# Where six modulation vectors of a two-layer trunk are made: one moves from attention into the channel mixer

## The chip, the cores and the metric

The kernel runs as one program on one core of a Trainium2 chip. The core has five instruction queues. TensorE (PE; its weight loads are listed apart as PEld) multiplies matrices and transposes. VectorE (DVE), ScalarE (ACT) and GpSimd (POOL) work element by element. SyncE (SP) issues nearly all transfers between the core and device memory. Each queue runs its instructions in the order in which they were put there, and an instruction that waits holds up everything behind it on its queue. The metric is the device time of one execution, in microseconds (us).

## What is computed

The reference is a trunk of two layers on a sequence of 1024 tokens and 1024 features. Each layer has a token mixer (layer 0: attention with a forget gate, 16 heads; layer 1: gated linear attention) and a channel mixer (SwiGLU with 2816 hidden features). Every part is normalised and then shifted, scaled and gated by six vectors, which come from one conditioning vector `c` and one matrix per layer:

```
c_act = silu(c)
for i in range(2):
    mod = c_act @ ada_w[i] + ada_b[i]            # 1024 x 6144 matrix, 24 MB per layer
    sh1, sc1, g1, sh2, sc2, g2 = split(mod, 6)   # six vectors of 1024
    h = rms_norm(x, norm1_g[i]) * (1 + sc1) + sh1
    y = attention(h) if i == 0 else gated_linear_attention(h)
    x = x + g1 * y
    h = rms_norm(x, norm2_g[i]) * (1 + sc2) + sh2
    gate, up = split(h @ ffn_w_in[i], 2)
    x = x + g2 * ((silu(gate) * up) @ ffn_w_out[i])
out = rms_norm(x, final_g)
```

This document numbers the vectors of a layer 0 to 5, as the code does (`j`): 0 and 1 are the first norm's shift and scale, 2 is the token mixer's gate, 3 and 4 are the second norm's shift and scale, 5 is the channel mixer's gate. "The sixth" is j = 5. The vectors depend on nothing but `c`, so they can be made at any time before their use.

## The kernel before

**Precision and tiling.** Every large product is made of three matmuls on float32r halves: a value is split in a high part (a ScalarE copy) and a low part (a VectorE or GpSimd subtraction), and `mm3` (lines 316 to 318) multiplies high by high, high by low and low by high. Activations lie with features on the 128 partitions and tokens along the free axis, in halves of 512 tokens. The two channel mixers use one level of Strassen's scheme (seven products instead of eight); a product there (`prod`) is twelve matmuls of 128x512.

**Attention of layer 0.** Eight pairs of heads, `p` = 0 to 7. While the scores, softmax and outputs of pair `p` run (`attention(p)`), the projections of pair `p+1` run between them: queries and keys (`qk_proj`, on TensorE `qk_b`) and, up to p = 5, values (`v_half`, `vps_b`). A generator pair is interleaved by given weights (`weave`), and a scheduler then puts the instructions on each engine's queue by its own estimate of times. In the softmax of one block of 128 queries, VectorE adds the gate sums and takes the minimum (line 1298), ScalarE exponentiates and sums (1302), VectorE takes the reciprocal of the sum (1303), GpSimd multiplies (1304), TensorE transposes (1324), ScalarE and VectorE split the transposed block (174, 175, `pt_s`), and TensorE multiplies it with the values (1338). VectorE also evacuates queries (869, 871) and keys (883, 884: `KLA`, `KLB`) and splits a quarter of the weights (246).

**How a modulation vector is made beside this work.** There are three makers, each a generator that is advanced a little at a time by a pacing counter (`Pace`):

- `ada_steps` with four tiles a step (attention): one step loads 512 KB of the matrix by four transfers of 128 KB (line 453) into a buffer of the ring `wr`, which the weights use too (three buffers), and VectorE multiplies and adds it to a sum in four instructions of 128x256 (line 516; the first of a vector is line 514). Eight steps make a vector. `ada0(t)` advances it by `t` steps after each of the projections `qk_proj` from p = 2 on.
- `ada_steps` with two tiles a step (channel mixers and the second token mixer): 256 KB by four transfers of 64 KB, two VectorE instructions of 128x256, sixteen steps a vector. A step costs `ADA_A + ADA_B` units of the counter, and each `prod` gives it 2.56. Buffers are its own: three of 256 KB in the channel mixers, with loads two steps ahead.
- `ada_pool` (attention): GpSimd makes one vector with a multiplication (477) and an addition (479) for each tile, from one buffer of its own.

At the end of a vector `ada_end` sums its parts by four small matmuls (459) on TensorE and adds the bias on VectorE (462). For j = 1 and 4, `make_a` then combines it with the norm's weight (444).

**Where the twelve vectors are made.** Layer 0: j = 0 and 1 at the start, j = 2, 3 and 4 by VectorE in attention, j = 5 by GpSimd in attention. Layer 1: j = 0 and 1 in the channel mixer of layer 0 (`mid(0, 1)`), j = 2, 3 and 4 in the gated linear attention, j = 5 in its own channel mixer. Layer 0's j = 2 is first used when attention's output is added to the stream (1442), j = 3 and 4 at the norm of the channel mixer, and j = 5 at the end of the channel mixer (1901 and 1928).

**The channel mixer's flow.** `mid()` is called once the two halves of the normalised input have been formed. Then twenty groups of seven products follow, each adding to running sums by VectorE (1670); five PSUM buffers take the products in turn, and the weights of up to five products ahead are split by ScalarE (174) and VectorE (175). Hidden values are split again (1548, 1549) and written out (1601) to be read back as tiles for the second matrix (1785). Before the last two groups `ada1.flush()` runs whatever is left of the vectors.

Of the kernel before, what the change touches and what calls it, by code (L numbers as in the profile page):

```python
# [53 lines left out]
def trunk(ctx, tc, x, c, ada_w, ada_b, norm1_g, norm2_g, ffn_w_in, ffn_w_out,  # L54
# [412 lines left out]
    def ada_pool(l, j, acc, raw):  # L467

        raw = raw.rearrange("p (t c) -> p t c", t=2)
        ada_load(raw, l, j, 0, 2)  # L470
        yield 1.0
        for n in range(16):
            for t in range(2):
                o = 32 + t * 16 + n
                y = raw[:, t] if n or t else acc
                with tc.issue_after(last_of("G")):
                    nc.gpsimd.tensor_scalar(y, raw[:, t], c42[:, o:o + 1], 1.0, op0=ALU.mult, op1=ALU.mult)
                    if n or t:
                        nc.gpsimd.tensor_add(acc, acc, y)
                if t and n < 15:  # L480
                    ada_load(raw, l, j, n + 1, 2)
                yield 1.0
        ada_end(l, j, acc)
        yield 1.0
# [61 lines left out]
    def ada1_queue(js, acc, raws_):  # L546
        r = Cycle(raws_)
        for j in js:
            ada1.q.append(ada_steps(1, j, acc, r, 2, len(raws_) - 1))

    mk = mrows[2]
    nc.vector.memset(mk, 0.0)
# [704 lines left out]
    def qk_proj(p, i):  # L1257

        if i == 0:
            qkt[p] = qk_tiles(p)  # L1260
        wt = feed.next()
        feed.depth = 3
        for hf in range(2):
            ps = pj([P, HALF], F32, f"qk{i}{p}{hf}")
            yield from proj(ps, wt, hT, hf)
            (k_evac if i else q_evac)(ps, qkt[p], hf)
        if p > 1:
            ada0(2.4)

    oTs = {}  # L1270

# [110 lines left out]
            yield from g  # L1382

    acc0 = acc_r([P, 2, HALF], F32, "acc0")
    ada0p.q.append(ada_pool(0, 5, acc0[:, 0, 256:512], acc0[:, 1]))
    acc0 = acc0[:, 0, 0:256]
    for j in (2, 3, 4):
        ada0.q.append(ada_steps(0, j, acc0, wr, 4, 0))
    run(v_half(0, 0, gates_end))
    q_evac(accs[1][1][1], qkt[0], 1)  # L1390
# [614 lines left out]
        ada1_queue(js, v[0][:, 0:256], v[1:4])  # L2005
        ada1.at -= 20.0

    ADA_A, ADA_B = 6.0, 3.0
    ffn(0, oh, xs, slots, "fo", lambda: mid(0, 1), norm_mixer)
    h1 = hs1  # L2010
    after_norm = marks.pop("G0")
    split_after.update(marks)
# [17 lines left out]
    athl = Ring(big, take(1))  # L2030
    s_slot, on_slot = take(2)
    ada_v = Views(take(2), 2, [HALF], "ad").v
    ada1_queue((2, 3, 4), ada_v[0][:, 0:256], ada_v[1:3])
    ADA_A, ADA_B = 2.6, 1.0
    nba = cst.tile([P, 4], F32, name="nba")
    nc.vector.tensor_scalar(nba, vec[:, P + 16:P + 20], -1.0, None, op0=ALU.mult)
# [494 lines left out]
        return fzs[hf]()  # L2531

    ADA_A, ADA_B = 12.0, 6.0
    ffn(1, None, xs, slots, "go", lambda: mid(5), final_norm, final_scale, (out_blocks, out_ends))
    dump("xb1", xs)

# [28 lines left out]
```

## Time and profile before

Three runs took 2346.65 us (median), 2345.26 and 2350.23. The profiled execution took 2348.03 us; its span from the first to the last instruction was 2346.3, so 1.7 us lie outside it. The granted TensorE clock was 0.995.

| Engine | busy, us | share of the span | instructions |
|---|---|---|---|
| TensorE (PE) | 2326.5 | 99% | 12168 |
| TensorE weight loads (PEld) | 1983.7 | 85% | 12168 |
| VectorE (DVE) | 1779.5 | 76% | 2947 |
| ScalarE (ACT) | 1123.0 | 48% | 2166 |
| GpSimd (POOL) | 1142.8 | 49% | 1005 |

Stages, by the instructions in the timeline: the start until about 125 us, attention of layer 0 until about 600, its channel mixer until about 1300, gated linear attention until about 1630, its channel mixer to the end.

A row of groups reads: line, engine, operation, tile written `<-` tiles read, shapes, count | busy time, mean ns of one | idle time of the engine just before them and what ended it. A row of waits reads: engine, line `<-` what it waited for: total us, how often, longest. A row of the timeline reads: start, duration, engine, line, operation, tiles, shapes, count, and in brackets the engine's idle time before it with what ended it. `SPq` is a transfer's issue. A row of stretches gives, for each engine, the busy time in that stretch and its instructions, then the granted clock, the DMA engines' busy share and GB/s.

### The profile page before, as it was taken

Reading aid. Unit: us, or ns where it says so; the run is one execution under the profiler, and the core shown is the slowest. Engines: PE = TensorE matmul, PEld = TensorE weight load, DVE = VectorE, ACT = ScalarE, POOL = GpSimd, SP = SyncE. Lnnn points to the kernel's source line nnn. Section 1 sums busy time; section 2 is a strip of 40 time slices with the busy share of each in tenths; the row PEclk is TensorE's granted clock in tenths of the full one; section 3 lists DMA queues with packets and bytes.
Section 4 is the critical chain, followed back from the end, with each engine's and each line's share of the span. In section 5 each row is a group of like instructions: output and inputs, shape, how many; then the busy total and the mean of one; then the engine's idle time right before and its main releaser. Section 6 shows DMA issues by size and latency. Waiting matters only on the chain.

```text
span 2346.3 us, 35561 instructions
## 1 busy us (share of the span) xinstructions
PE 2326.5 (99%) x12168; PEld 1983.7 (85%) x12168; DVE 1779.5 (76%) x2947; ACT 1123.0 (48%) x2166; POOL 1142.8 (49%) x1005
## 2 busy tenths in 40 slices
PE   8999999999999999999999999999999999999999
PEld 7988888888888888888888899898888888888888
DVE  6577787877687888887788666568787777876787
ACT  6565665665544333345325654345444333345236
POOL 1334455533345656665563522335456666664651
PEclk8999999999999999999999999999999999999999
DMA  8423333432325545448774443554435544458774
GB/s 262 146 79 116 108 113 94 128 127 103 117 95 188 184 162 167 161 172 314 253 272 155 134 129 100 148 174 167 150 106 160 177 150 156 140 189 299 238 267 137
DMA packets 349615, 383.38 MB, mean 163 GB/s; under 512 B 25373, under 2 KB 286649, under 8 KB 349433
## 3 DMA queue, kind: packets, MB, share of 16 engines
q1 hardware_dynamic: 349432, 381.11, 49.3%
q8 instruction: 96, 1.57, 0.3%
q14 instruction: 87, 0.70, 0.1%
HBM read 279.76 MB, written 101.25 MB: 162 GB/s over the span
## 4 chain that ended last, share of the span: by engine, by line
PE 90%; DVE 3%; DMA 3%; issue 1%; SPq 1%; ACT 1%; POOL 1%; DVEq 0%; POOLq 0%; ACTq 0%
PE p_b L316 16%; PE p_b L318 16%; PE p_b L317 16%; PE o_b L1338 2%; PE t_b L1324 2%; PE qk_b L316 2%; PE qk_b L317 2%; PE qk_b L318 2%; PE vps_b L318 1%; PE vps_b L316 1%; PE vps_b L317 1%; PE gr_b L316 1%; PE s_b L1292 1%; PE s_b L1293 1%; PE gr_b L317 1%
## 5 line engine op out<-in xcount | busy, mean ns | idle before, releaser
L174 ACT CAST o_s<-xv_s 128x512 fp32r<-128x512 f32 (+1 forms) x392 | 236.5, 610 | 344.4 <-PE p_b L318 256.9
L175 DVE TENSOR_TENSOR o_s<-xv_s,o_s 128x512 fp32r<-128x512 f32 (+1 forms) x392 | 335.2, 860 | 42.6 <-ACT o_s L174 40.5
L318 PE MATMUL p_b<-B,o_s 128*128 128x512 f32 x608 | 236.0, 389 | 0.0
L317 PE MATMUL p_b<-B,o_s 128*128 128x512 f32 x608 | 235.9, 389 | 0.0
L316 PE MATMUL p_b<-B,o_s 128*128 128x512 f32 x608 | 235.4, 390 | 0.0
L1304 POOL TENSOR_SCALAR lp_s<-lp_s,st 128x128 f32<-128x128 f32 (+7 forms) x128 | 98.2, 771 | 246.1 <-DVE st L1303 231.2
L951 POOL TENSOR_TENSOR ex_s<-xv_s,xv_s 128x512 f32<-128x512 f32 (+1 forms) x64 | 95.6, 1494 | 238.3 <-DMA xv_s<-in_ffn_w_in_dram 118.4
L316 PE MATMUL p_b<-T,o_s 128*128 128x512 f32 x480 | 186.8, 389 | 0.0
L317 PE MATMUL p_b<-T,o_s 128*128 128x512 f32 x480 | 186.7, 389 | 0.0
L318 PE MATMUL p_b<-T,o_s 128*128 128x512 f32 x480 | 181.2, 389 | 0.0
L318 PEld LDWEIGHTS p_b<-B,o_s 128*128 128x128 f32 x608 | 114.1, 188 | 23.9
L316 PEld LDWEIGHTS p_b<-B,o_s 128*128 128x128 f32 x608 | 114.1, 188 | 23.7 <-DVE x L1670 0.2
L317 PEld LDWEIGHTS p_b<-B,o_s 128*128 128x128 f32 x608 | 114.2, 188 | 23.5
L1302 ACT ACTIVATE lp_s<-lp_s,st 128x128 f32<-128x128 f32 (+7 forms) x128 | 99.4, 777 | 57.2 <-DVE st L1298 55.8
L953 POOL TENSOR_TENSOR xv_s<-ex_s,xv_s 128x512 f32<-128x512 f32 (+1 forms) x64 | 94.5, 1477 | 58.9 <-DVE o_s L175 55.9
L1670 DVE TENSOR_TENSOR ex_s<-ex_s,p_b 128x512 f32<-128x512 f32 x140 | 94.2, 681 | 36.7 <-PE p_b L318 36.6
L174 ACT CAST pt_s<-t_b 128x512 fp32r<-128x512 f32 (+1 forms) x160 | 79.7, 547 | 73.7 <-PE t_b L1324 73.1
L963 POOL TENSOR_TENSOR xv_s<-xv_s,xv_s 128x512 f32<-128x512 f32 x48 | 65.5, 1365 | 92.7 <-issue 52.3
L246 POOL TENSOR_TENSOR w_l_s<-w__s,w_h_s 128x256 fp32r<-128x256 f32 x90 | 69.4, 800 | 84.3 <-ACT w_h_s L242 66.3
L175 DVE TENSOR_TENSOR pt_s<-t_b,pt_s 128x512 fp32r<-128x512 f32 (+1 forms) x160 | 96.3, 630 | 15.9 <-ACT pt_s L174 15.4
L318 PEld LDWEIGHTS p_b<-T,o_s 128*128 128x128 f32 x480 | 90.1, 188 | 18.7
L317 PEld LDWEIGHTS p_b<-T,o_s 128*128 128x128 f32 x480 | 90.1, 188 | 18.7
(1527 smaller groups left out, 7413.9 us busy)
## 6 DMA issues: line engine op xcount, KB each, us to landing
xv_s<-in_ffn_w_in_dram SPq DMA_DIRECT2D x176, 256.0 KB, 3.2
hid_B<-x SPq DMA_DIRECT2D x66, 512.0 KB, 2.8
ad_s<-in_ada_w_dram SPq DMA_DIRECT2D x384, 64.0 KB, 2.4
hid_T<-x SPq DMA_DIRECT2D x44, 512.0 KB, 2.9
xv_s<-in_ffn_w_out_dram SPq DMA_DIRECT2D x88, 256.0 KB, 3.8
ada_s<-in_ada_w_dram SPq DMA_DIRECT2D x96, 128.0 KB, 2.7
T2o<-hid_T SPq DMA_DIRECT2D x22, 512.0 KB, 6.6
T1o<-hid_T SPq DMA_DIRECT2D x22, 512.0 KB, 6.3
```

What stands on the lines that cost most here:

```text
L174: nc.scalar.copy(hi, src)
L175: nc.vector.tensor_sub(lo, src, hi.bitcast(F32))
L246: (nc.gpsimd if i < 3 else nc.vector).tensor_sub(lo[:, cs], rw[:, cs], hi[:, cs].bitcast(F32))
L316: nc.tensor.matmul(ps, ah, bh, start=start, stop=False, skip_group_check=chain)
L317: nc.tensor.matmul(ps, ah, bl, start=False, stop=False, skip_group_check=chain)
L318: nc.tensor.matmul(ps, al, bh, start=False, stop=stop, skip_group_check=chain)
L951: nc.gpsimd.tensor_add(s1, a21, a22)
L953: nc.gpsimd.tensor_sub(a11, s1, a11)
L963: nc.gpsimd.tensor_sub(r[A12], r[A12], r[A11])
L1302: nc.scalar.activation(lp, lp, AF.Exp, bias=mcur, scale=-1.0, accum_out=st[:, qi, 2:3])
L1304: nc.gpsimd.tensor_scalar(lp, lp, st[:, qi, 3:4], 1.0, op0=ALU.mult, op1=ALU.mult)
L1670: nc.vector.tensor_add(d, d if src is None else dest(G, src), ps)
```

## The change

Layer 0's j = 5 is no longer made in attention. GpSimd makes j = 4 there in its place, by the same instructions, and VectorE makes only j = 2 and 3, at 1.6 steps per call where it had 2.4. The channel mixer of layer 0 makes three vectors where it had made two: layer 0's j = 5 first, then layer 1's j = 0 and 1. A step's price there falls from 6 + 3 to 4 + 2 units, so that 48 steps take as many units (288) as 32 did. The argument of `mid` and `ada1_queue` now counts over both layers (5 is layer 0's j = 5; 6 and 7 are layer 1's 0 and 1), which is all that the other two places of the diff say.

```diff
@@ ada1_queue
-            ada1.q.append(ada_steps(1, j, acc, r, 2, len(raws_) - 1))
+            ada1.q.append(ada_steps(*divmod(j, 6), acc, r, 2, len(raws_) - 1))
@@ qk_proj
         if p > 1:
-            ada0(2.4)
+            ada0(1.6)
@@ before the attention
-    ada0p.q.append(ada_pool(0, 5, acc0[:, 0, 256:512], acc0[:, 1]))
+    ada0p.q.append(ada_pool(0, 4, acc0[:, 0, 256:512], acc0[:, 1]))
     acc0 = acc0[:, 0, 0:256]
-    for j in (2, 3, 4):
+    for j in (2, 3):
         ada0.q.append(ada_steps(0, j, acc0, wr, 4, 0))
@@ channel mixer of layer 0
-    ADA_A, ADA_B = 6.0, 3.0
-    ffn(0, oh, xs, slots, "fo", lambda: mid(0, 1), norm_mixer)
+    ADA_A, ADA_B = 4.0, 2.0
+    ffn(0, oh, xs, slots, "fo", lambda: mid(5, 6, 7), norm_mixer)
@@ gated linear attention
-    ada1_queue((2, 3, 4), ada_v[0][:, 0:256], ada_v[1:3])
+    ada1_queue((8, 9, 10), ada_v[0][:, 0:256], ada_v[1:3])
@@ channel mixer of layer 1
-    ffn(1, None, xs, slots, "go", lambda: mid(5), final_norm, final_scale, (out_blocks, out_ends))
+    ffn(1, None, xs, slots, "go", lambda: mid(11), final_norm, final_scale, (out_blocks, out_ends))
```

The scheduler places the rest of attention anew around the missing steps, so the order of instructions moves there on all engines. Three places follow, all on VectorE.

The first is in attention, where the queries of pair 6 are about to be evacuated (the reciprocal at its end belongs to a block of 640 keys). `ada_s` are the loaded pieces of the matrix, `acc_s` the sum, `lp_s` the scores, `st` their minimum and sum, `pt_s` the transposed block. Before:

```order
L175 TENSOR_TENSOR pt_s_94_4711<-t_b_94_4706,pt_s_94_4711 128x512
L516 SCALAR_TENSOR_TENSOR acc_s_1_749<-ada_s_45_4791,c_164,acc_s_1_749 128x256 x3
L516 SCALAR_TENSOR_TENSOR acc_s_1_749<-ada_s_47_5084,c_164,acc_s_1_749 128x256 x4
L1298 ISA lp_s_62_4758,st_4760<-s_b_117_4761,cum_s_10_4058 128x384
L1298 ISA st_4760 128x1
L175 TENSOR_TENSOR pt_s_95_4728<-t_b_95_4724,pt_s_95_4728 128x384
L1298 ISA lp_s_62_4758,st_4760<-s_b_118_4765,cum_s_10_4058,st_4760 128x256
L1298 ISA st_4760 128x1
L516 SCALAR_TENSOR_TENSOR acc_s_1_749<-ada_s_48_5093,c_164,acc_s_1_749 128x256
L175 TENSOR_TENSOR pt_s_96_4823<-t_b_96_4818,pt_s_96_4823 128x512
L516 SCALAR_TENSOR_TENSOR acc_s_1_749<-ada_s_48_5093,c_164,acc_s_1_749 128x256
L1303 RECIPROCAL st_4760<-st_4760 128x1
```

Now:

```order
L175 TENSOR_TENSOR pt_s_94_4666<-t_b_94_4661,pt_s_94_4666 128x512
L1298 ISA lp_s_62_4713,st_4715<-s_b_117_4716,cum_s_10_4013 128x384
L1298 ISA st_4715 128x1
L1298 ISA lp_s_62_4713,st_4715<-s_b_118_4720,cum_s_10_4013,st_4715 128x256
L1298 ISA st_4715 128x1
L175 TENSOR_TENSOR pt_s_95_4683<-t_b_95_4679,pt_s_95_4683 128x384
L1303 RECIPROCAL st_4715<-st_4715 128x1
```

Nine instructions of the modulation vector (three, four, one and one) have left the queue ahead of the reciprocal.

The second is one pair of heads later, where keys are evacuated (`KLA`, `KLB`) and the first weights of attention's output matrix are split (`wo_0l_s`). Before:

```order
L516 SCALAR_TENSOR_TENSOR acc_s_1_749<-ada_s_56_5927,c_164,acc_s_1_749 128x256 x2
L1303 RECIPROCAL st_5377<-st_5377 128x1
L516 SCALAR_TENSOR_TENSOR acc_s_1_749<-ada_s_56_5927,c_164,acc_s_1_749 128x256
L1298 ISA lp_s_73_5441,st_5442<-s_b_139_5443,cum_s_12_4846 128x384
L1298 ISA st_5442 128x1
L246 TENSOR_TENSOR wo_0l_s_54_5650<-wo_0_s_54_5647,wo_0h_s_53_5649 128x256
L883 TENSOR_TENSOR KLA_4859<-qk_b_42_5481,KA_4857 64x512
L884 TENSOR_TENSOR KLB_4860<-qk_b_42_5481,KB_4858 64x512
L1298 ISA lp_s_73_5441,st_5442<-s_b_140_5451,cum_s_12_4846 128x512
```

Now:

```order
L1303 RECIPROCAL st_5319<-st_5319 128x1
L1298 ISA lp_s_73_5383,st_5384<-s_b_139_5385,cum_s_12_4788 128x384
L1298 ISA st_5384 128x1
L246 TENSOR_TENSOR wo_0l_s_54_5592<-wo_0_s_48_5589,wo_0h_s_53_5591 128x256
L1298 ISA lp_s_73_5383,st_5384<-s_b_140_5393,cum_s_12_4788 128x512
L1298 ISA st_5384 128x1
L883 TENSOR_TENSOR KLA_4801<-qk_b_41_5423,KA_4799 64x512
L884 TENSOR_TENSOR KLB_4802<-qk_b_41_5423,KB_4800 64x512
```

The vector's instructions are gone here too (eight in this stretch, of which the last three are shown), and the scores of the next block now stand ahead of the evacuation of the keys.

The third is in the channel mixer of layer 0, within one group of seven products. `ad_s` are the loaded pieces and the sum, `o_s` the split weights, `p_b` the products. Before:

```order
L1549 TENSOR_TENSOR x_4_6281<-sg_s_7621,x_4_6281 128x512
L516 SCALAR_TENSOR_TENSOR ad_s_7895<-ad_s_7895,c_164 128x256
L1670 TENSOR_TENSOR x_1_6278<-x_0_6277,p_b_33_8636 128x512
L175 TENSOR_TENSOR o_s_47_8675<-xv_s_7380,o_s_47_8675 128x512
L516 SCALAR_TENSOR_TENSOR ad_s_7895<-ad_s_7895,c_164 128x256
L1670 TENSOR_TENSOR x_0_6277<-x_0_6277,p_b_30_8566 128x512
```

Now, at the same product:

```order
L516 SCALAR_TENSOR_TENSOR ad_s_7819<-ad_s_7819,c_164 128x256 x2
L516 SCALAR_TENSOR_TENSOR ad_s_7819<-ad_s_7820,c_164,ad_s_7819 128x256
L1670 TENSOR_TENSOR x_1_6202<-x_0_6201,p_b_33_8582 128x512
L516 SCALAR_TENSOR_TENSOR ad_s_7819<-ad_s_7820,c_164,ad_s_7819 128x256
L175 TENSOR_TENSOR o_s_47_8623<-xv_s_7304,o_s_47_8623 128x512
L1670 TENSOR_TENSOR x_0_6201<-x_0_6201,p_b_30_8508 128x512
```

Four of the vector's instructions stand around this product, up to three in a row, where two stood apart.

## The prediction

> **What bounds the kernel now.** I read the page first, then each stage as a stretch, then who keeps TensorE waiting.
>
> ```profile
> PE 2326.5 (99%) x12168; PEld 1983.7 (85%) x12168; DVE 1779.5 (76%) x2947; ACT 1123.0 (48%) x2166; POOL 1142.8 (49%) x1005
> L318 PE MATMUL p_b<-B,o_s 128*128 128x512 f32 x608 | 236.0, 389 | 0.0
> ...
> 125.00:560.00 435.00, 430.17 (x2790) 377.81 (x2789) 338.79 (x857) 269.43 (x575) 197.56 (x283) 1.00 0.36 114
> 560.00:720.00 160.00, 160.00 (x786) 133.89 (x785) 121.37 (x200) 78.10 (x140) 67.23 (x58) 1.00 0.33 109
> 720.00:1022.00 302.00, 302.00 (x1336) 250.10 (x1335) 252.99 (x325) 113.61 (x197) 189.28 (x127) 1.00 0.51 169
> ```
>
> TensorE is busy for 2326.5 of 2346.3 us. The change removes no matmul, so time can come only from the gaps in TensorE's work. The stage that the change relieves (125 to 560 us, attention) holds 435.00 - 430.17 = 4.8 us of them. The stage that it loads (720 to 1022, the products of the channel mixer) holds none: any gap there would be new. A gap costs a little more than the idle time shown, because matmuls overlap: one is listed with 389 ns, yet in the channel mixer 302.00 us / 1336 = 226 ns separate two starts. So 0.16 us (389 - 226) of each stall hides under the tail of the matmul before it.
>
> Who ends the gaps in attention (waits of TensorE, 100 to 600 us):
>
> ```profile
> PE t_b L1324 <- POOL lp_s L1304: 2.7, 2, 2.0
> PE qk_b L316 <- DVE QB L871: 1.1, 2, 0.5
> PE fo010p_b L316 <- DVE x L1442: 0.3, 1, 0.3
> PE o_b L1338 <- DVE pt_s L175: 0.3, 1, 0.3
> PE s_b L1292 <- DVE st L1298: 0.3, 1, 0.3
> PE t_b L1324 <- DVE pt_s L175: 0.2, 1, 0.2
> ```
>
> The list names some eight stalls, 4.9 us together; with 8 x 0.16 = 1.3 hidden, about 6.1 us is all that attention can give. That is 0.26% of the time, and about 0.2% (4.7 us) is what a measurement of this kernel can tell from no change.
>
> **The largest stall, followed back.** One wait of 2.0 us stands out. The timeline around it, by engine (TensorE, GpSimd, ScalarE, VectorE, SyncE):
>
> ```profile
> 412.30 0.23 PE L1295 MATMUL s_b<-maskb,identb 128*128 128x128 bf16 x1
> 414.50 0.55 PE L1324 MATMUL t_b<-ident,lp_s 128*128 128x128 f32 x3 [1.97 <-POOL lp_s L1304]
> ...
> 413.50 0.95 POOL L1304 TENSOR_SCALAR lp_s<-lp_s,st 128x640 f32<-128x640 f32 x1 [9.03 <-DVE st L1303]
> ...
> 411.32 0.19 ACT L1302 ACTIVATION_READ_ACCUMULATOR lp_s<-lp_s,st 128x1 f32 x1
> ...
> 407.10 2.04 DVE L516 SCALAR_TENSOR_TENSOR acc_s<-ada_s,c,acc_s 128x256 f32<-128x256 f32 x4 [0.20 <-DMA ada_s<-in_ada_w_dram]
> 410.41 0.08 DVE L1298 DVE_READ_ACCUMULATOR2_ANT st<- 128x1 f32 x1
> 411.78 0.48 DVE L516 SCALAR_TENSOR_TENSOR acc_s<-ada_s,c,acc_s 128x256 f32<-128x256 f32 x1 [1.29 <-DMA ada_s<-in_ada_w_dram]
> 413.17 0.15 DVE L1303 RECIPROCAL st<-st 128x1 f32<-128x1 f32 x1
> ...
> 401.37 8.04 SPq L453 DMA_DIRECT2D ada_s<-in_ada_w_dram  x8
> ```
>
> GpSimd waited 9.03 us for the reciprocal. The sum that it needs was there at 411.32 + 0.19 = 411.51, but the reciprocal ran at 413.17, since VectorE stood from 410.49 to 411.78 in front of a piece of the modulation matrix that had not landed. Before that, seven pieces in a row (the x4 of 407.10 and three ahead of it) had pushed the scores of this very block back. So this stall is made by the pieces that the change thins out, and the changed order (first place shown above) has none of them ahead of that reciprocal.
>
> **The change, part by part, in attention.** The cost of a vector on VectorE (a group of 125 to 520 us, and a row of the loaded tile's own view):
>
> ```profile
> L516 DVE SCALAR_TENSOR_TENSOR acc_s<-ada_s,c,acc_s 128x256 f32<-128x256 f32 x93 | 51.1, 549 | 16.0 <-DMA ada_s<-in_ada_w_dram 14.3
> ...
> L514 DVE TENSOR_SCALAR acc_s<-ada_s,c x3: 589/745/752, 140.5 to 398.4; 128x256 f32<-128x256 f32 x3
> ```
>
> I call one such instruction a piece; four make a step, 32 a vector.
>
> One vector of three goes: 31 x 0.549 + 0.745 = 17.8 us of work and a third of the 16.0 us of waiting, 5.3. VectorE falls from 338.79 to about 321 busy in 435 us. This is not time gained: it counts only where TensorE was waiting.
>
> - *The stall at 414.5*: 1.97 + 0.16 = 2.1 us. I take all of it, **-2.1**; bounds 0 (the wait reappears at another reciprocal) and -2.1.
> - *The stalls of the next pair* (469 to 493 us): the two of `qk_b` and the two of `pt_s`, 1.1 + 0.3 + 0.2 + 4 x 0.16 = 2.2 us. Their stretch begins so:
>
> ```profile
> 449.46 2.40 DVE L516 SCALAR_TENSOR_TENSOR acc_s<-ada_s,c,acc_s 128x256 f32<-128x256 f32 x4 [2.19 <-DMA ada_s<-in_ada_w_dram]
> 462.74 0.78 DVE L246 TENSOR_TENSOR wo_0l_s<-wo_s,wo_0h_s 128x256 fp32r<-128x256 f32 x1
> 465.13 0.68 DVE L883 TENSOR_TENSOR KLA<-qk_b,KA 64x512 fp32r<-64x512 f32 x1 [1.61 <-ACT KB L882]
> 466.55 0.69 DVE L1298 CUSTOM_DVE_ANT_0 lp_s<-s_b,cum_s 128x512 f32<-128x512 f32 x1
> 468.75 1.89 DVE L175 TENSOR_TENSOR pt_s<-t_b,pt_s 128x512 fp32r<-128x512 f32 x3 [0.45 <-ACT pt_s L174]
> ```
>
>   Eight pieces leave this stretch (8 x 0.549 = 4.4 us), but from 463.5 to 465.1 VectorE waited for ScalarE, so part of the lateness was not VectorE's load. The changed order puts the scores ahead of that wait (second place above). Bounds 0 and -2.2; I take half, **-1.1**.
> - *The loads*: eight steps' transfers (32 of 128 KB) leave SyncE's queue and the ring that the weights share; what follows (weights, reloaded attention outputs) can only come earlier. The waits of TensorE on weights or transfers in attention have no row, so **0**.
> - *GpSimd's vector* runs the same instructions for j = 4 as for j = 5; nothing changes but the due time. **0**.
> - *The new order itself*: every engine's queue is placed anew in attention, and a new stall can arise. The nearest price is the stall just followed, 2.1 us; the best case is none. I take **+0.4**, a fifth of it, since 16 of 24 steps remain and before the change they gave one such stall in 24.
>
> **In the channel mixer.** What 32 more instructions and 64 more transfers of 64 KB meet there (720 to 1022 us; the two tile rows 690 to 1030):
>
> ```profile
> L516 DVE SCALAR_TENSOR_TENSOR ad_s<-ad_s,c,ad_s 128x256 f32<-128x256 f32 x37 | 21.0, 568 | 0.3
> L516 DVE SCALAR_TENSOR_TENSOR ad_s<-ad_s,c 128x256 f32<-128x256 f32 x18 | 10.3, 570 | 0.1
> L1670 DVE TENSOR_TENSOR ex_s<-ex_s,p_b 128x512 f32<-128x512 f32 x55 | 36.8, 679 | 3.6 <-PE p_b L318 3.6
> ...
> DVE x L1549 <- ACT x L1548: 32.1, 19, 3.9
> DVE x L1670 <- PE p_b L318: 7.1, 5, 2.5
> ...
> L516 DVE SCALAR_TENSOR_TENSOR ad_s<-ad_s,c,ad_s x41: 469/474/1511, 734.6 to 1018.6; 128x256 f32<-128x256 f32 x41
> L453 SPq DMA_DIRECT2D ad_s<-in_ada_w_dram x120: 560/585/1927, 689.5 to 987.2; - x120
> ```
>
> VectorE gains 32 x 0.568 = 18.2 us and stands at 252.99 + 18.2 = 271 of 302 us (90%). It still has 31 us left, and it is the one that waits today: for ScalarE (32.1 us) and for TensorE's products (7.1 in the row shown). Its adds may fall behind by four products before a PSUM buffer is missing: 4 x 12 matmuls x 0.226 = 10.8 us. Runs of pieces in the new order are up to four long (where a vector starts), 2.3 us. So the cover is VectorE's own slack, and the cost is **0**. If the cover were gone, the price would be the whole 18.2 us, which is the upper bound. SyncE issues 64 x 0.585 = 37 us more in 302 us, 4 MB more moved; a piece is loaded two steps ahead, and a step is now 6 / 2.56 x 2.71 = 6.4 us, so it has over 12 us for four issues (2.3 us) and a landing. Cost **0**. The vector's end costs TensorE four small matmuls in either place: **0**.
>
> The sum is -2.1 - 1.1 + 0.4 = **-2.8 us** on the profiled execution's 2348.03, so 2345.2. That execution lies 1.4 us above the median of the three runs (2346.65), and from the median it is 2343.9; I predict **2344 us**. Attention's terms at their bounds reach from -4.3 to +2.1.
>
> [...]
>
> **Rivals.**
>
> 1. *The waits only move.* Two thirds of the steps stay, their four pieces in a row in places, and VectorE still stands in front of pieces that have not landed (16.0 us over three vectors, so 10.7 for two). The stall at 414.5 is gone, another of its size takes its place: -1.1 - 1.0 + 2.1 = 0, so 2346.7. For it: the row at 449.46, where a piece waited 2.19 us. Against it: 24 steps made only one large stall.
> 2. *All of attention's VectorE stalls go*: -6.1 us, 2340.6, faster by 0.26%. For it: five of the six rows name VectorE directly and the sixth, GpSimd's, stands for its reciprocal. Against it: one is at the seam to the output projection, after the last step, and VectorE idles in front of others.
> 3. *A slower one: the steps that remain sit in front of the keys.* The scheduler now puts eight pieces between two evacuations of keys in the pair before (`L516` one by one, then three, then one, ahead of `L883`): 8 x 0.549 = 4.4 us. The keys hold one of the two PSUM buffers of the projections, so TensorE's next projection would wait. It decides once the keys are late by more than the other buffer's projection takes (24 matmuls x 0.226 = 5.4 us). With a transfer that lands 2.2 us late, as at 449.46, they are 6.6 us late, which costs 1.2 us. At three such places and with nothing else gained it is +3.6, 2350.2.
> 4. *A slower one in the channel mixer.* If GpSimd blocks most pieces, old and new, VectorE becomes the bound. It has 302 - 253 + 31.3 (the 55 pieces in the rows) = 80.3 us for 55 + 32 = 87 of them, 0.92 us each; the mean is 0.57, the longest 1.51. At a mean of 1.04 it is 87 x 0.12 = +10 us, 2357. [...] GpSimd is busy 189 of 302 us there, which speaks for it; that 62 pieces now have a median of 474 ns speaks against it.
>
> **How the numbers follow.** My forecast 50%, rival 1 22%, rival 2 14%, rival 3 9%, rival 4 3%, and 2% that TensorE gains more than attention's listed idle time. The likeliest case's own range is 2341.5 to 2346. For 8 in 10 the range must reach into rivals 1 and 2, and medians of three runs lie 1 to 2 us apart (2345.26 to 2350.23 before): **2340 to 2348.5**. Faster by over 0.2% means below 2342: most of rival 2 and a tail of the forecast, 0.18. Slower by over 0.2% means above 2351.3: rival 4 and part of rival 3, 0.05. Within 0.2%: 0.77.
>
> **What would show it.** In the changed profile attention's TensorE idle time (125 to 560) should fall from 4.8 to about 2.3 us, and GpSimd's longest wait for the reciprocal below 9.03. The row of `L516` on `acc_s` should have 62 pieces, and its wait on transfers should be about 11 us. The channel mixer's stretch should keep 302.00 busy of 302.00 with VectorE near 271. I am wrong if a wait of TensorE shows up between 690 and 1030 us, if the listed stalls of attention stay as they are with the steps gone, or if the gain is larger than 6 us.

## The result, and the profile after

The changed kernel takes **2353.22 us** (median of 19 runs, 2349.47 to 2355.68), the kernel before 2347.34 in the same comparison (19 runs, 2344.39 to 2350.5). The ratio is **1.0021, 95% interval 1.0015 to 1.0028**: slower by 5.9 us, where I forecast 2344 in a range of 2340 to 2348.5. The profiled execution took 2351.04 us, 2.2 below its kernel's median, and the one before, 2348.03, lay 0.7 above its own: the two traces differ by 3.0 us and show about half of the loss.

The views of the prediction, for the changed kernel. First the stretches of attention and of the channel mixer (busy time of TensorE, weight loads, VectorE, ScalarE, GpSimd):

```profile
125.00:560.00 435.00, 431.24 (x2793) 377.96 (x2792) 324.84 (x826) 270.89 (x577) 198.89 (x285) 1.00 0.33 104
720.00:1022.00 302.00, 299.10 (x1318) 245.83 (x1317) 277.30 (x349) 111.14 (x194) 187.60 (x126) 1.00 0.55 179
```

Attention's idle time fell from 4.8 to 3.8 us. The channel mixer, which had none, has 2.9, and in the same 302 us TensorE starts 1318 matmuls where it started 1336: 18 x 0.226 = 4.1 us of work are missing. VectorE is busy for 277.3 us there, not for the 271 that I had worked out.

Who makes TensorE wait, first in attention (125 to 560 us; the first two of five rows), then from 690 to 1030 us, where the list was empty before:

```profile
PE vps_b L316 <- DVE QB L871: 1.2, 1, 1.2
PE qk_b L316 <- DVE QB L871: 1.1, 2, 0.5
```

```profile
PE p_b L316 <- DVE x L1670: 1.8, 2, 1.2
PE mp_b L459 <- DVE ad_s L516: 1.1, 2, 0.6
```

GpSimd's stall of 2.0 us is gone from attention, a new one of 1.2 is there. In the channel mixer TensorE waits for VectorE's adds (line 1670) and, in the four small matmuls that end a vector, for the last piece.

What VectorE does in the channel mixer (groups, 720 to 1022 us), before and after. The prediction's two rows of pieces end at 1000 us and count 55; over the whole stretch there were 61.

```profile
L516 DVE SCALAR_TENSOR_TENSOR ad_s<-ad_s,c,ad_s 128x256 f32<-128x256 f32 x41 | 23.9, 582 | 0.3
...
L516 DVE SCALAR_TENSOR_TENSOR ad_s<-ad_s,c 128x256 f32<-128x256 f32 x20 | 12.7, 634 | 0.1
```

```profile
L516 DVE SCALAR_TENSOR_TENSOR ad_s<-ad_s,c,ad_s 128x256 f32<-128x256 f32 x58 | 39.1, 675 | 0.6
...
L516 DVE SCALAR_TENSOR_TENSOR ad_s<-ad_s,c 128x256 f32<-128x256 f32 x30 | 24.1, 802 | 0.3
```

It is not only that 27 pieces were added. The mean of all of them rose from (23.9 + 12.7) / 61 = 0.60 to (39.1 + 24.1) / 88 = 0.72 us. One by one, 6 of 61 took over 1.3 us before, 19 of 88 after, and each of these 25 ended 0.28 to 0.29 us after an instruction of GpSimd's. The timeline ahead of the first stall shows how (VectorE, GpSimd and the TensorE matmul that had to wait):

```profile
779.62 1.56 DVE L1549 TENSOR_TENSOR x<-sg_s,x 128x512 fp32r<-128x512 f32 x1
781.10 2.95 DVE L516 SCALAR_TENSOR_TENSOR ad_s<-ad_s,c 128x256 f32<-128x256 f32 x2
784.49 0.68 DVE L1670 TENSOR_TENSOR x<-x,p_b 128x512 f32<-128x512 f32 x1
...
786.09 0.68 DVE L1670 TENSOR_TENSOR x<-x,p_b 128x512 f32<-128x512 f32 x1
...
788.01 0.67 DVE L1670 TENSOR_TENSOR x<-x,p_b 128x512 f32<-128x512 f32 x1
...
789.61 0.67 DVE L1670 TENSOR_TENSOR x<-x,p_b 128x512 f32<-128x512 f32 x1
...
779.01 1.62 POOL L1630 TENSOR_TENSOR sg_s<-sg_s,sg_s 128x512 f32<-128x512 f32 x1
780.71 1.62 POOL L1635 TENSOR_TENSOR sg_s<-sg_s,sg_s 128x512 f32<-128x512 f32 x1
782.41 1.36 POOL L1639 TENSOR_TENSOR sg_s<-sg_s 128x512 f32<-128x512 f32 x1
...
790.34 0.50 PE L316 MATMUL p_b<-B,o_s 128*128 128x512 f32 x1 [0.67 <-DVE x L1670]
```

The two pieces at 781.10 take 2.95 us, 1.5 each instead of 0.48. Each ends about 0.3 us after an instruction of GpSimd's (782.33 and 783.77). The four adds behind them, and what stands between, follow without a pause of VectorE's, and the matmul at 790.34 starts 0.06 us after the fourth has ended (789.61 + 0.67 = 790.28; 0.05 before rounding). Before the change the same place read:

```profile
782.83 1.56 DVE L1549 TENSOR_TENSOR x<-sg_s,x 128x512 fp32r<-128x512 f32 x1
784.32 0.47 DVE L516 SCALAR_TENSOR_TENSOR ad_s<-ad_s,c 128x256 f32<-128x256 f32 x1
...
788.51 0.67 DVE L1670 TENSOR_TENSOR x<-x,p_b 128x512 f32<-128x512 f32 x1
...
782.22 1.63 POOL L1639 TENSOR_TENSOR sg_s<-sg_s 128x512 f32<-128x512 f32 x1
...
790.57 0.39 PE L316 MATMUL p_b<-B,o_s 128*128 128x512 f32 x1
```

There one piece stood alone behind GpSimd's run and took 0.47 us, and the add had ended at 789.18, **1.39 us** ahead of the matmul.

**Why this add, and not one four products back.** The queue order of the changed kernel says it (TensorE's rows first, then VectorE's; the numbers in front give the order within a queue, `p0_b2_30` is product 30 in PSUM bank 2):

```
3989 L316 MATMUL p0_b2_30_8508<-T100_7555,o003s_s22_38_8406 128x512
...
4096 L316 MATMUL p0_b2_35_8627<-B2200_7547,o00301_s21_43_8524 128x512

1201 L516 SCALAR_TENSOR_TENSOR ad5_s48_7819<-ad5_s48_7819,c42_164 128x256 x2
1202 L516 SCALAR_TENSOR_TENSOR ad5_s48_7819<-ad5_s49_7820,c42_164,ad5_s48_7819 128x256
1203 L1670 TENSOR_TENSOR x0_1_6202<-x0_0_6201,p0_b0_33_8582 128x512
...
1206 L1670 TENSOR_TENSOR x0_0_6201<-x0_0_6201,p0_b2_30_8508 128x512
...
1208 L1670 TENSOR_TENSOR x0_1_6202<-x0_1_6202,p0_b1_34_8602 128x512
...
1211 L1670 TENSOR_TENSOR x0_1_6202<-x0_1_6202,p0_b2_30_8508 128x512
```

Of the seven products of a group, the one with T1 is added twice, into C12 and into C22, and keeps its bank until the second add, the last of four behind one another. Five banks go round, so the group's last product (with B22) needs exactly this bank. The time between the two, from the trace with the products told apart by the queue order (start of B22's first matmul, less the end of T1's second add), I call the **margin**. In every second group, where GpSimd runs a chain of five or six instructions for the hidden values, it is small:

| product B22, number | 21 | 35 | 49 | 63 | 77 | 91 | 105 | 119 |
|---|---|---|---|---|---|---|---|---|
| before, us | 1.31 | 1.39 | 1.65 | 1.44 | 1.78 | 1.24 | 1.45 | 0.60 |
| after, us | 0.21 | 0.05 | 0.06 | 0.12 | 0.06 | 0.05 | 0.75 | 0.41 |

In the groups between these it is 2.5 to 4.4 us before, 1.1 to 3.6 after. (The first group, product 7, has 0.15 us in both; its B22 starts before the first piece.) At 0.05 to 0.06 the matmul starts right behind the add: at products 35 and 91 TensorE is idle for 0.67 and 1.17 us in front of it, while at 77 and 49 its start is late by 0.15 us or less, hidden under the matmul before. So the cover of the channel mixer was 0.6 to 1.8 us in every second group, not the 10.8 of four products.

### The profile page after: what moved, and what is told of

It reads as the page before. It is cut to its first block, busy times and chain, and to the rows that moved or that the text cites. A ratio compares the mean times of both kernels' runs of the same rounds, so it can differ in the third digit from the quotient of the medians.

```text
span 2349.3 us, 35606 instructions
## 1 busy us (share of the span) xinstructions
PE 2329.5 (99%) x12168; PEld 1984.6 (84%) x12168; DVE 1789.0 (76%) x2947; ACT 1122.7 (48%) x2166; POOL 1143.7 (49%) x1005
## 4 chain that ended last, share of the span: by engine, by line
PE 56%; DVE 4%; DMA 2%; issue 2%; POOL 2%; ACT 0%; SPq 0%; DVEq 0%; POOLq 0%
PE p_b L316 11%; PE p_b L317 11%; PE p_b L318 11%; PE gr_b L316 1%; PE gr_b L317 1%; PE gr_b L318 1%; PE gv_b L316 1%; PE gv_b L318 1%; PE gv_b L317 1%; DVE ad_s L516 1%; DVE o_s L175 1%; PE gqp_b L318 1%; DMA ex_s<-hid_T 1%; PE gk_b L316 1%; PE gqp_b L316 1%
## 5 line engine op out<-in xcount | busy, mean ns | idle before, releaser
L175 DVE TENSOR_TENSOR o_s<-xv_s,o_s 128x512 fp32r<-128x512 f32 (+1 forms) x392 | 340.3, 873 | 45.4 <-ACT o_s L174 44.8
L1298 DVE CUSTOM_DVE_ANT_0 lp_s<-s_b,cum_s 128x512 f32<-128x512 f32 (+3 forms) x128 | 72.6, 569 | 44.9 <-PE t_b L1324 22.0
L316 PEld LDWEIGHTS p_b<-T,o_s 128*128 128x128 f32 x480 | 90.1, 188 | 18.6
```

The source lines that it names most:

```text
L175: nc.vector.tensor_sub(lo, src, hi.bitcast(F32))
L316: nc.tensor.matmul(ps, ah, bh, start=start, stop=False, skip_group_check=chain)
L1298: nc.vector.tensor_tensor_reduce(lp[:, k0:k1], ps, cm[:, k0:k1], 1.0, mcur, ALU.add, ALU.min, mnew)
```

## The experiments

My theory, P in the expectations: the extra pieces are held up by GpSimd, VectorE's adds come later than the queue order allows for, and TensorE loses time where the margin is used up. The rivals: O, attention's new order costs more than its trace shows; S, SyncE's 64 more issues and the 4 MB moved; W, the mere number of pieces, or their standing in a row, without GpSimd. Times below are differences of medians to the kernel before, run in the same comparison.

### Each half of the change alone

Attention's half, with the mixer as before (layer 0's sixth vector is not made at all, its bias stands in), and the mixer's half on top of the old attention (the first diff is to the changed kernel; the second shows what differs from the one before, the numbering of the vectors aside):

```diff
-    ADA_A, ADA_B = 4.0, 2.0
-    ffn(0, oh, xs, slots, "fo", lambda: mid(5, 6, 7), norm_mixer)
+    ADA_A, ADA_B = 6.0, 3.0
+    def mid_two():
+        nc.vector.tensor_copy(modc[:, 0, 5], vec[:, 40:48])
+        mid(6, 7)
+    ffn(0, oh, xs, slots, "fo", mid_two, norm_mixer)
```

> Only attention's half of the change: GpSimd makes j = 4, VectorE j = 2 and 3, in the changed kernel's order up to the channel mixer; the mixer makes two vectors at 6 and 3 units as before. Layer 0's sixth vector is left out: its bias alone stands in. [...] Rival O (the new order in attention costs more than its profile shows): +3 us or more. [...]

```diff
-    ADA_A, ADA_B = 6.0, 3.0
-    ffn(0, oh, xs, slots, "fo", lambda: mid(0, 1), norm_mixer)
+    ADA_A, ADA_B = 4.0, 2.0
+    ffn(0, oh, xs, slots, "fo", lambda: mid(5, 6, 7), norm_mixer)
```

> Only the channel mixer's half: attention as before (GpSimd makes j = 5 there too, VectorE three vectors), and the mixer makes three vectors at 4 and 2 units, j = 5 a second time. So it does 32 pieces more in all. Theory P: the changed kernel's loss without its gain in attention, 5.9 + 1.5 = about +7 us over before, with the stalls of TensorE behind VectorE in the mixer as in the changed kernel (some 3 to 5 us of idle time from 720 to 1022 us). Rival O: about 0. S and W as P.

Attention's half: 2347.11 against 2348.62 us, ratio 0.9992 (0.9983 to 1.0), -1.5 us. The mixer's half: 2354.87, 1.0024 (1.0015 to 1.0033), +6.3 us. The stretch of the channel mixer in the first, then in the second:

```profile
720.00:1022.00 302.00, 302.00 (x1337) 250.22 (x1336) 253.39 (x328) 114.36 (x199) 190.10 (x128) 1.00 0.52 171
```

```profile
720.00:1022.00 302.00, 297.31 (x1307) 243.77 (x1306) 275.00 (x348) 109.72 (x192) 185.31 (x125) 1.00 0.54 176
```

The halves add up to 4.8 us, near the 5.9 of the whole. O falls: the loss is made in the channel mixer, and attention gives what its trace shows.

### The pieces without GpSimd in their way

The running sum of a vector goes to a PSUM bank, so that a piece has one input in SBUF instead of two (dots stand for lines that are not shown, here and below):

```diff
+                    run_ = acc if accp is None else accp
+                    to = acc if n == 32 // nt - 1 and t == nt - 1 else run_
...
-                        nc.vector.scalar_tensor_tensor(acc, raw[:, t], c42[:, o:o + 1], acc,
+                        nc.vector.scalar_tensor_tensor(to, raw[:, t], c42[:, o:o + 1], run_,
                                                       op0=ALU.mult, op1=ALU.add)
...
```

> The changed kernel, but in the channel mixer of layer 0 the running sum of a vector lies in a PSUM bank (one of the three that the first layer's second-matrix products and rms sums had as reserve) and only the last piece writes it to SBUF. So 95 of 96 pieces read one input from SBUF and one from PSUM. Theory P: the pieces are no longer held up by GpSimd, their mean falls from 0.72 to about 0.5 us and their longest from 1.52 to under 0.7, VectorE's busy time in 720 to 1022 us falls from 277 to about 265, the waits of TensorE for VectorE there go, and the time is that before less attention's gain, -1 to -2 us (up to +1 if the lost bank costs anything). W and S: the time stays like the changed kernel's, +5 to +6 us.

2346.79 against 2348.62 us, 0.9994 (0.9986 to 1.0003), **-1.8 us**: the whole loss is gone and attention's gain is left. The stretch, and the pieces (the view of the tile: least, median and longest in ns):

```profile
720.00:1022.00 302.00, 302.00 (x1338) 250.12 (x1337) 256.68 (x357) 114.94 (x199) 186.07 (x127) 1.00 0.56 182
```

```profile
L518 DVE SCALAR_TENSOR_TENSOR adp<-ad_s,c,adp x90: 474/478/491, 712.6 to 1021.3; 128x256 f32<-128x256 f32 x90
```

Not one of 90 pieces takes longer than 491 ns, where the changed kernel's longest took 1520; the list of TensorE's waits from 690 to 1030 us is empty again, and none of the eight margins is under 1.17 us. The transfers and the number of pieces are the same, so S and the first form of W fall here. VectorE's busy time falls too, to 256.7 us; the last run below separates the two. GpSimd is busy for 186.1 of the 302 us here and for 187.6 in the changed kernel, so it is not a quieter GpSimd that spares the pieces. Why a sum in PSUM spares them, these runs do not show.

### The two pieces of a step apart

The pieces stay in SBUF, but the second of a step comes 3 units after the first (3 + 3 units a step, as 4 + 2 before):

```diff
                 for t in range(nt):
+                    if t and spread:
+                        es.close()
+                        yield spread
+                        es.enter_context(tc.issue_after(last_of("D")))
...
```

> The changed kernel, but the two pieces of a step stand apart in the channel mixer of layer 0 (3 units between them, at most the same mean pace). Theory W's second form (pieces in a row are what makes the adds late): most of the loss goes, +1 us or less over before. Theory P (each piece is held up by GpSimd wherever it stands): the loss stays for the most part, +3 to +6 us, with a mean piece of 0.7 us. Rival O: +5 to +6.

2348.36 against 2348.62, 1.0002 (0.9993 to 1.0011), -0.3 us. I had expected the loss to stay for the most part. It went, as W's second form had said, though the pieces are held up as before and VectorE is nearly as busy:

```profile
720.00:1022.00 302.00, 301.88 (x1334) 249.18 (x1333) 274.48 (x354) 112.91 (x198) 188.91 (x127) 1.00 0.55 182
```

```profile
L521 DVE SCALAR_TENSOR_TENSOR ad_s<-ad_s,c,ad_s 128x256 f32<-128x256 f32 x60 | 44.0, 734 | 0.2
...
L521 DVE SCALAR_TENSOR_TENSOR ad_s<-ad_s,c 128x256 f32<-128x256 f32 x30 | 21.5, 717 | 0.1
```

The mean is 0.73 us, the same as in the changed kernel. The margins of the eight groups are 0.64, 0.51, 0.06, 0.05, 0.79, 1.78, 0.88 and 0.12: used up, but hardly overdrawn. So the sum of held-up time alone does not make the loss. In the sums in PSUM the pieces stand in a row and nothing is lost; here they are held up, but apart, and at most a small part of the loss is left (-0.3, where attention's half alone gives -1.5). What fits both is that it costs where held-up time falls together in front of those adds.

### Transfers, pace, and the ends of vectors

Three more edits: the changed kernel with 52 of the added transfers left out and all pieces kept (layer 0's sixth vector is then summed from its first three loads again and again); attention's half from above, with its two vectors in the mixer at the changed kernel's pace (the second diff is to that kernel); the changed kernel with the end of a vector put one product later.

```diff
             n = steps.popleft()
+            if (l, j) == (0, 5) and n >= 3:
+                got.append(kept[n % 3])
+                return
...
```

> The changed kernel with all 96 pieces in the channel mixer of layer 0, but without 52 of the 64 added transfers: layer 0's sixth vector is summed over its first three loaded steps again and again, so that vector is wrong. Theory P (pieces held up by GpSimd, two or more in a row, make VectorE's adds late, and TensorE runs out of PSUM buffers): the loss stays, +4 to +6 us, with waits of TensorE for VectorE's adds (line 1670's) and for the ends of vectors between 690 and 1030 us. Rival S (SyncE's 64 more issues or the transfers' share of the DMA engines): most of the loss goes, +1 or less.

```diff
-    ADA_A, ADA_B = 6.0, 3.0
+    ADA_A, ADA_B = 4.0, 2.0
     def mid_two():
```

> Attention's half alone again (layer 0's sixth vector left out, its bias stands in), but the channel mixer's two vectors are made at the changed kernel's pace of 4 and 2 units: 64 pieces as before, crowded into the first two thirds. If the loss comes from how many pieces stand in a row or near each other (local), two thirds of it: the stalls near 790 and 823 us are there, and one near 920; the time is +1 to +3 us over before, against -1.5 of the same kernel at the old pace. If it comes from VectorE's total (253 against 277 us of 302), nothing: -1.5 us.

```diff
             yield ADA_B if ahead else 1.0
+        if ahead == 2:
+            yield 2.5
         ada_end(l, j, acc)
```

> The changed kernel with the four small matmuls that end a vector in the channel mixer put one product (2.5 units) later, so that they should no longer stand in TensorE's queue ahead of VectorE's last piece. The two waits for the last piece (1.1 us shown, 1.4 with the hidden part) should go: +3 to +5 us over before. If the loss hung on these ends alone (the last piece held up, TensorE's queue standing in front of it): +1 or less.

Without the transfers: 2352.06 us, 1.0017 (1.0008 to 1.0025), +3.4. The loss stays for the most part, a little under the 4 to 6 that I had written. Its interval (1.9 to 5.9 us) overlaps that of the changed kernel (3.5 to 6.6), so this run alone leaves room for a share of S; the sums in PSUM, with every transfer, leave none.

Two vectors at the faster pace: 2351.2 us, 1.0011 (1.0002 to 1.002), **+2.5**, against -1.5 at the old pace. VectorE is busy for only 258.6 of 302 us here, and TensorE waits (690 to 1030 us; the first of three rows):

```profile
720.00:1022.00 302.00, 298.86 (x1316) 245.51 (x1315) 258.56 (x326) 112.92 (x196) 189.75 (x126) 1.00 0.51 171
```

```profile
PE p_b L316 <- DVE sg_s L1670: 1.9, 2, 1.1
```

The last piece runs at 920 us; the margins are 0.05 to 0.15 in the six groups to 946 us, and 3.12 in the next. With the 61 pieces of before, 13 now take over 1.3 us, and the mean is (25.8 + 17.1) / 61 = 0.70 us. So the loss is local: it follows the density of the pieces, not their number in the stage.

The later ends: 2353.64 us, 1.0023 (1.0014 to 1.0032), +5.0. The waits for the last piece fell from 1.1 to 0.3 us, but those for the adds rose from 1.8 to 4.6, so nothing is won. The time that TensorE lost at one place it lost at the next.

### More banks

If the margin at one bank is what costs, more banks should heal it with the pieces left as they are. Six banks in the ring, then two banks of their own for the T1 products, each with its control on the kernel before:

```diff
-        pin, pj = Ring(psp, bk[:5]), Ring(psp, bk[5:])
+        six = 6 if l == 0 else 5
+        pin, pj = Ring(psp, bk[:six]), Ring(psp, bk[six:])
```

> The changed kernel with six PSUM banks in place of five for the channel mixer's products in layer 0 (one of the three reserve banks joins them). The pieces stay as they are, in SBUF, held up by GpSimd. In the profiles before and after, the product B22 of each group starts at the bank that the group's product T1 held until its second add (the one into C22), and before the change that add ended only 1.3 to 1.8 us ahead of B22 in every other group; after it, 0.05 to 0.2. Theory P in its present form (VectorE's delay shows where it passes this margin): with a sixth bank the margin is a product or more (2.7 us) wider, the waits of TensorE from 690 to 1030 us go though the mean piece stays near 0.7 us and VectorE near 275 us; time -1 to -2 us under before, and the interval below the changed kernel's. If VectorE were short of time over the whole stage, the sixth bank would only put the waits off: +4 us or more.

> Control: the kernel before with the same six banks. Its channel mixer has no wait to take away, so within 1 us of the time before by every theory. If it gains 2 us or more, six banks help for another reason than the added pieces, and the other run shows less than it seems to.

```diff
-        pin, pj = Ring(psp, bk[:5]), Ring(psp, bk[5:])
+        pin, pj = Ring(psp, bk[:5]), Ring(psp, bk[5:] if l else bk[7:])
+        own = pin if l else Ring(psp, bk[5:7])
...
-            p5 = prod(feed.next(), T1)
+            p5 = prod(feed.next(), T1, own)
```

> The changed kernel, but the product T1 of each group in the channel mixer of layer 0, whose bank is held until its second add, takes turns on two reserve banks of its own; the other six products keep the five banks. So no product starts at a bank that is freed only by the second add of T1, which with five or six shared banks was the one that TensorE stood in front of. The pieces stay in SBUF, held up by GpSimd. Theory P (VectorE's delay costs through this one bank): no wait of TensorE for line 1670 between 690 and 1030 us, the mean piece still 0.65 us or more and VectorE at 270 us or more, and the time at -1 to -2 us against the one before. If VectorE has too little time over the whole stage: another bank's wait takes its place, +4 us or more. The ends of vectors (up to 1.4 us) may stay by either.

> Control: the kernel before with the same two banks of its own for T1. Nothing waits in its channel mixer, so within 1 us of the time before.

Both of my expectations were wrong, and by much. Six banks: 2363.3 us, 1.007 (1.0058 to 1.0083), +15.4. Own banks: 2363.69, 1.0064 (1.0051 to 1.0076), +15.2. The controls: 2349.95, 1.0009 (1.0 to 1.0018), +2.1, and 2347.98, 0.9997 (0.9987 to 1.0006), -0.5. With six banks the T1 product's bank goes to the next group's first product, and TensorE waits for the same second add there (0.05 us of margin at products 22, 36, 64, 78, 92, 106 and 120); in the control, too, that margin is 0.05 us at 22 and 64. With own banks the waits for adds are gone but for 0.4 us, as meant, and the ends of vectors take their place, at 824.78 and 1036.79 us (waits of TensorE, 690 to 1330 us):

```profile
PE mp_b L459 <- DVE ad_s L516: 11.9, 2, 6.4
PE p_b L316 <- DVE x L1670: 0.4, 1, 0.4
```

and the pieces are held up more (groups, 720 to 1022 us), at a mean of (45.4 + 28.0) / 86 = 0.85 us:

```profile
L516 DVE SCALAR_TENSOR_TENSOR ad_s<-ad_s,c,ad_s 128x256 f32<-128x256 f32 x58 | 45.4, 782 | 0.5
...
L516 DVE SCALAR_TENSOR_TENSOR ad_s<-ad_s,c 128x256 f32<-128x256 f32 x28 | 28.0, 1002 | 0.4
```

The same order of products on the kernel before, without a vector more, raises its mean from 0.60 to (32.9 + 18.6) / 62 = 0.83 us. Yet this control is not slower: no margin of its products is under 3.6 us between 690 and 1100 us. With a cover that wide the dearer pieces cost nothing here (-0.5 us). An edit of the banks makes the order on all engines anew; that this puts more pieces beside GpSimd's instructions is my estimate from the two means, and was not followed piece by piece in these kernels. What a waiting product had hidden came out too: TensorE, no longer held back by banks, ran 6.4 us ahead of VectorE's pieces until the end of the vector stopped it.

The last edit of this line puts those ends three products later and starts the vectors four products earlier:

```diff
+        if l * 6 + j in (5, 6, 7):
+            yield 7.7
         ada_end(l, j, acc)
...
-        ada1.at -= 20.0
+        ada1.at -= 10.0
```

> The previous kernel of this series (the changed one, T1 on two banks of its own) with the four small matmuls that end a vector put three products later (7.7 units) and the three vectors begun four products earlier to make room. In that previous kernel the waits for banks were gone but for 0.4 us, and three waits for the last piece of a vector, 6.4, 5.5 and 5.5 us, had taken their place, with a granted clock of 0.57 to 0.74 for some 8 us behind the first. Theory P (VectorE is behind the order only for a time, and what it costs is set by the few places where TensorE's queue stands in front of it): most of those waits go, time -1 to +3 us against the one before. If VectorE is behind more and more through the stage (277 of 302 us busy is too much in the end): the waits come back at the moved ends or at other banks, +8 us or more.

(That text counts three waits, where the row above has two; and 0.57 and 0.74 were the clocks with six banks, with own banks they were 0.62 and 0.70.) 2359.92 us, 1.0044 (1.003 to 1.0058), +10.5. The waits at the ends are gone, TensorE is full to 860 us, and then waits for banks come back, 1.5 us at 861.50 and 1.8 us at 901.63 (the first three of eight rows, 690 to 1330 us; the second row is a wait for a transfer, after 1080 us):

```profile
PE p_b L316 <- DVE sg_s L1672: 2.0, 2, 1.8
PE p_b L316 <- DMA T2o<-hid_T: 1.5, 2, 1.2
PE p_b L316 <- DVE x L1672: 1.5, 1, 1.5
```

The pieces take (46.0 + 21.6) / 80 = 0.85 us on average. The least margin of any product falls from 6.2 us (700 to 740 us) over 3.1 and 1.5 to 0.15 from 860 us on, and stays under 0.3 until 1060: in this kernel VectorE falls behind by more and more, and more buffering only moves the place where it is noticed. The next run asks whether the changed kernel, with 0.72, is short in the same sense.

### The same time on VectorE, nothing held up

The kernel with the sums in PSUM, and after each piece one more VectorE instruction whose result nobody reads:

```diff
+                        if accp is not None:
+                            nc.vector.tensor_scalar(spare, raw[:, t, 0:112], c42[:, o:o + 1], None, op0=ALU.mult)
...
```

> The kernel with the running sums in PSUM, but after each piece VectorE also multiplies 112 columns of the loaded tile into an unused part of the same bank (one input from SBUF, result not used), so that a piece with its addition takes about 0.72 us, as much as a piece held up by GpSimd took on average in the changed kernel, yet never 1.5 us at once. VectorE should be busy 275 to 280 us of 302. Theory P with sums (the time that VectorE lacks is what costs, wherever it falls): the loss is back, +4 to +6 us, with waits of TensorE for line 1672's adds. Theory P with lumps (pieces of 1.5 us, two in a row, just ahead of the adds that TensorE waits for): -2 to +1 us, little or no wait. The order is made anew with the added instructions in its estimate, which speaks for a smaller loss by both.

2347.54 against 2348.51 us, 0.9995 (0.9986 to 1.0004), **-1.0 us**. The stretch, and the two instructions of a piece:

```profile
720.00:1022.00 302.00, 302.00 (x1337) 250.21 (x1336) 278.41 (x446) 114.80 (x198) 189.12 (x128) 1.00 0.56 182
```

```profile
L523 DVE TENSOR_SCALAR adp<-ad_s,c x93: 321/330/340, 714.8 to 1027.0; 128x112 f32<-128x112 f32 x93
L520 DVE SCALAR_TENSOR_TENSOR adp<-ad_s,c,adp x90: 474/483/491, 714.3 to 1023.0; 128x256 f32<-128x256 f32 x90
```

VectorE is busy for 278.4 us, more than the 277.3 of the changed kernel, and TensorE waits for nothing; the eight margins are 1.6 us or more. So 92% of VectorE's time does no harm where no piece is held up. With the pieces apart (274.5 us, no loss) and two vectors at the faster pace (258.6 us, a loss), this says that VectorE's total is not what cost in the changed kernel.

What stays open: this order was made anew with the added instructions in the scheduler's estimate, as the order of the pieces apart was. Whether the held-up pieces hurt because they are long where they fall (1.5 us, two in a row, ahead of the critical adds) or because the scheduler's estimate knew nothing of their length, these runs do not tell apart: none has held-up pieces with their true length in that estimate.

## Why the prediction was wrong, step by step

**The stall at 414.5: right.** It is gone, and its place shows nothing. TensorE's idle time of attention fell by 1.0 us, and attention alone, timed, gave -1.5 against the forecast -2.8. The interval of that run, -4 to 0 us, holds both.

**The next pair's stalls: -0.5 instead of -1.1.** `qk_b <- QB` stands at 1.1 us as before. Of the two waits on `pt_s` the one at 469.50 (0.3 us, with its hidden part 0.5) is gone and the other stays, so -0.5 came of the forecast -1.1.

**The new order: right in kind, short in size.** A new stall of 1.2 us came (`vps_b <- QB`, at 300.12), with its hidden part 1.4, where I had taken 0.4 out of a bound of 2.1. By the trace the three terms give -2.1 - 0.5 + 1.4 = -1.2 us, near the -1.5 that was timed.

**The vector's rows in attention: right.** The group of 125 to 520 us has 62 pieces and waits 11.4 us for transfers, as I had written (62 and about 11):

```profile
L516 DVE SCALAR_TENSOR_TENSOR acc_s<-ada_s,c,acc_s 128x256 f32<-128x256 f32 x62 | 38.0, 613 | 12.4 <-DMA ada_s<-in_ada_w_dram 11.4 <-DVE st L1303 0.3
```

**SyncE and the transfers at 0: right**, by the sums in PSUM, which kept all of them and lost nothing.

**"So the cover is VectorE's own slack, and the cost is 0": this step failed**, and with it the sign. It measured +6.3 us. Three things were wrong in it.

- *The price of a piece.* I took 0.568 us for the added ones, from rows that end at 1000 us (over the whole stretch the mean was 0.60). It came out as 0.72 for all, and VectorE at 277.3 us instead of 271: more of the pieces fell into GpSimd's chain, 19 of 88 instead of 6 of 61, up to 1.5 us each. A mean that holds waiting inside it does not stay when more is put there.
- *The distance to harm.* I had "four products, 10.8 us" from the number of banks. The trace before already showed 1.39 us at one place, where the add at 788.51 frees the bank of the matmul at 790.57. I counted buffers, and did not ask which of them was held longest.
- *Slack taken from a sum.* 31 us of VectorE's 302 were idle, and I spent them as if they lay where the pieces would. The run at 278.4 us without loss and the run at 258.6 with one show that this sum did not decide it.

**The vector's end at 0: wrong by about 1.4 us** (1.1 shown, and twice 0.16 hidden), though moving it won nothing.

**Rival 4 had half of the mechanism**, and I gave it 3%. GpSimd did stand in the way, though of 19 pieces in 88 and not of most; its point of decision was not reached. I had put that at 0.92 us for each piece, where VectorE would be full; the loss was there at 0.72, with 25 us of VectorE idle. What I held against it, a median piece of 474 ns, is still true (480 and 485 ns after the change): the median says nothing of the fifth that is held up.

**Rival 1's sum** does not follow from the terms: the stall at 414.5 gone, another of its size come and the next pair's -1.1 make -1.1, not 0. It changes nothing in what failed.

**What would show it: that part worked.** A wait of TensorE between 690 and 1030 us was the sign I named for being wrong, and it is the one that came.

## What to carry to other kernels

Before work is put on an engine that "has slack", look up in the trace, for each place where the bounding engine depends on it and the new work will stand ahead, how long the awaited instruction had been done: the smallest of those times is the cover, not the idle sum and not the count of buffers (in this kernel, the buffer that is read twice was held longest). When an instruction's longest time is three times its median, as the pieces' was (1511 against 474 ns), find out what held the long ones; price added ones at the long value where they will meet it, or try other operands and see whether the long ones go. Here the sum in PSUM did that (491 ns at most, against 1520): it takes back the whole loss of the change (-1.8 us to the kernel before, against +5.9). It can't be told from the kernel before (0.9986 to 1.0003), so no gain of the change is shown even then.

## What the runs showed that I had not expected

**A stall of 6.36 us cost more than its length.** In the kernel with own banks TensorE waited 6.36 us for the end of a vector, and the granted clock (last figure but two) was low in the 5 us after it:

```profile
824.78 1.02 PE L459 MATMUL mp_b<-four,ad_s 128*128 128x4 f32 x4 [6.36 <-DVE ad_s L516]
```

```profile
820.00:825.00 5.00, 0.22 (x1) 0.70 0.75 262
825.00:830.00 5.00, 5.00 (x17) 0.62 0.49 179
830.00:835.00 5.00, 5.00 (x24) 1.00 0.42 133
```

From 825 to 830 us 17 matmuls were started, the small ones among them, where 24 go otherwise, though TensorE is listed as busy throughout. The eight large ones from 825.66 to 829.05 took 3.39 us, where eight starts otherwise take 8 x 0.226 = 1.81: 1.6 us more. The 2.0 us of attention's old stall left the clock at 1.00, and around the end of a stall of 4.0 us (with six banks) it was 0.57 over 5 us. What lowers the clock, and from what length of a stall on, these runs do not show.

**More buffers made it slower.** With one bank more the kernel lost 15.4 us instead of 5.9. Its order was made anew, its pieces took 0.79 us on average, and TensorE waited for 4.0 us at the end of a vector where it had waited 0.6 at most; how the 9.5 us divide among these was not measured. An edit that only relieves can change the order on every engine, and its control (the same edit without the change, +2.1 us) belongs to it.
